# Trunk of two layers: substitution tile in PSUM, six general PSUM banks, products of constants in the heads, and a finish that keeps its split weights

## The chip, the core and the metric

The kernel runs on one core of a Trainium2 chip. PE is the matrix engine (TensorE), DVE the vector engine, ACT the scalar engine, POOL is GpSimd, and SP issues most of the transfers (DMA). Time is device microseconds (us) of one launch. PSUM is the small memory that PE writes its products to, here eight banks of 128 x 512 floats; SBUF is the large working memory. [...]

## The reference, cut to what matters

```
for i in range(2):                                   # two layers
    hx, hc = modulate(rmsnorm(x)), modulate(rmsnorm(ctx))      # 1024 latent, 256 context tokens
    fx, fc = hx @ w_in[i], hc @ w_in[i]
    att_x = softmax attention of 8 heads, 1280 keys            # group A
    y = bidirectional RWKV-7 scan of 8 heads of 64             # group B
        # state = state * w + (state a) b^T + v k^T ;  y = state r
    x = x + gate * (concat(att, rwkv) @ w_out[i])
    x = x + gate * (square(relu(modulate(rmsnorm(x)) @ w_mlp1[i])) @ w_mlp2[i])
return rmsnorm(x, final_g)
```

All numbers are float32. The scan is computed in ten steps of 128 tokens for both directions at once. Within a block of 64 tokens it needs the inverse of 32 unit triangular matrices, whose 32 x 32 parts come out of a forward substitution.

## The kernel before

Each layer has three parts: `phase_in` (input projections, per-token terms), `heads` (the scan and the attention, interleaved) and `phase_out` (output projection and the MLP). In the profile below the heads of layer 0 run from about 504 to 1171 us, those of layer 1 from about 2621 to 3266 us.

**The planner.** Nothing in a part is in hand-written order. Each piece of work is a unit (`us(engine, ns, dependencies, function, ...)`) of the class `Units`, with a duration on its engine, a latency until others may use its result, perhaps a PSUM bank, and the number of PE rows it uses. `run` simulates the engines with these numbers: at each turn it takes, of the units that could start within `slack` of the earliest, the one with the longest path behind it, where `RANKS_HEADS` adds an offset to named kinds of unit. It also models PE's clock, from how much PE was used. The order so found is the order of the instructions on each engine; at run time each engine then runs its queue strictly in that order and waits where an operand is late. So the planner's numbers choose an order and are no times of the chip.

**A bank class** is a list of PSUM tiles that units draw from. Before, the heads have `g` (3 banks: score products, blocks, transposes, small sums), `x` (2: products for the row maxima), `z` (2: the chain of the scan's state) and `o` (1: attention output), together eight.

**The recurrence.** Step i loads `BV` and `AR`, forms blocks on PE (L377) that DVE masks into `A` (L381), transposes tokens (L391, L401), and ACT moves them (`BKt`, `G`). `begin1` to `begin3` lay the 32 triangular matrices out in `AX` and make unit rows in `Y` (`begin2b`, two kinds of POOL memset). The substitution is 31 turns of two DVE instructions: `mult` (L436) writes `tmp` from a column of `AX` and a row of `Y`, `total` (L440) adds `tmp` into `Y`. Each needs the one before. `AX`, `Y` and `tmp` all lie in SBUF. `end1` to `end3` carry the result to `XT`, after which PE and ACT run the chain z, u, s, y (L519 to L562) for each half of a step and direction.

**The attention** takes per head and 512 queries twelve products for the row maxima (L715, reduced by DVE at L717), the negated maximum (L718) spread by PE (L723), ten times three score products (L742), exponentials on ACT (L747), sums on POOL (L751), and products with the values (L736).

**The finish.** The last part of the last layer multiplies the last quarter of hidden units (four weight tiles `R[0]` to `R[3]`) into `x` for the first 512 tokens (a = 1), then for two pieces of 256 (a = 2), and normalises. Weights go to PE as two rounded parts: `split_weights` rounds on ACT (L967) and subtracts the rest on DVE or, for a = 2, on POOL (L969). It does so again for each piece, twelve splits in all. `hh` and `hl`, 16 tiles that hold the split input of the MLP, are idle after the last hidden product.

Of the kernel before, what the change touches and what calls it, by code (L numbers as in the profile page):

```python
# [9 lines left out]
F32 = mybir.dt.float32  # L10
# [89 lines left out]
def sp_ns(n, k=1):  # L100
# [16 lines left out]
class Units:  # L117
# [5 lines left out]
    WINDOW, UP, DOWN = 3413.3, 0.83, 0.47  # L123

    def __init__(self, slack, ranks, latency={}, give_back=True, cold=False, up=UP, down=DOWN, lead=0):
# [37 lines left out]
    def run(self, banks):  # L163
# [21 lines left out]
        while waiting:  # L185
# [11 lines left out]
            ns = u.ns + (u.beside if free.get("Pool", 0.0) > s else 0)  # L197
            if u.eng == "PE":
# [64 lines left out]
class Trunk:  # L263
# [34 lines left out]


    def heads(self, li, ard, bvd, pc, gated, ysd, kd, vd, qd, qrd, krr, catd):  # L300

        with ExitStack() as es:
            e1 = self.pool(es, "hd", 1)
            ps = self.pool(es, "hps", 1, space=PSUM)
            banks = {k: [ps.tile([128, 512], F32, name=f"ps_{k}{j}") for j in range(n)] for k, n in (("g", 3), ("x", 2), ("z", 2), ("o", 1))}
            tiles = {}


            for name, n, shape in (("YF", 1, [128, 32, 32]), ("AX", 1, [128, 32, 32]), ("XM", 1, [128, 32, 32]), ("Y", 1, [128, 32, 16]), ("tmp", 1, [128, 144]),
# [6 lines left out]
            us = Units(59, RANKS_HEADS, dict(PE=120, ACT=75, DVE=75, Pool=75, SP=2300), False, True, 0.745, 0.395, 100)  # L316
# [6 lines left out]
    def recurrence(self, us, tiles, li, ard, bvd, pc, gated, ysd, catd):  # L323
# [9 lines left out]
        YF, XT, XM, tmp, sq, rs8 = (tiles[k][0] for k in ("YF", "XT", "XM", "tmp", "sq", "rs8"))  # L333
# [3 lines left out]
        half = lambda e: slice(64 * e, 64 * e + 64)  # L337
        heads = [(p, e, half(e)) for p in range(4) for e in range(2)]
# [11 lines left out]
        def step(i):  # L350
# [20 lines left out]
            for d in range(2):  # L371
                for ph in range(2):
                    for e in range(2):
# [9 lines left out]
                        x = add(f"blk{d}", us("PE", 772, back(NA, "begin", "m1", "z0", "z1", "y0", "y1"), pe, 284, bank="g", r=[nar[d], nbv[d]], rows=61))  # L383
                        add("A", us("DVE:A", 707, [x], dve, free=x))


            for d in range(2):
                for ph in range(2):
# [7 lines left out]
                    x = add(f"tok{d}", us("PE", 470, [], pe, 213, bank="g", r=[nbv[d]], rows=121))  # L396
# [10 lines left out]
                x = add(f"tok{d}", us("PE", 480, [], pe, 213, bank="g", r=[nbv[d]], rows=121))  # L407
# [3 lines left out]
            for h in range(2):  # L411
                def begin1(h=h):
                    q = slice(32 * h, 32 * h + 32)
                    nc.scalar.copy(YF[q].rearrange("p t n -> p n t"), A[64 + 32 * h:96 + 32 * h, :, 0, q])

                add("begin", us("ACT:begin1", 1970, w["A"] + back(1, "begin2"), begin1))
# [12 lines left out]
            b2 = us("DVE", 1261, w["begin"] + back(NX, "end3"), begin2)  # L429
            b2b = us("Pool", 907, back(NY, "end1"), begin2b)  # L430
# [31 lines left out]
            e2 = add("end2", us("DVE", 1994, e1s + back(1, "m1", "x2"), end2))  # L462
            e2b = add("end2", us("DVE", 1266, e1s, end2b))
            e3b = [add("end3", us("ACT:end3", 1970, [e2b] + back(2, "u0", "u1") + zero, lambda j=j: end3b(j))) for j in (1, 0)]
# [16 lines left out]
            for d in range(2):  # L481
# [9 lines left out]
                x = add("x2", us("PE", 570, [m1a[d], e3b[0]], pe, bank="g", rows=15))  # L491
# [18 lines left out]
            for c in range(2):  # L510
                for d in range(2):
# [52 lines left out]
                    x = add(f"z{d}", us("PE", 567, copies[d] + [az[d]] + w["A"][4 * d:4 * d + 4] + w[f"V{d}"], z_pe, 138, bank="z", rows=121))  # L564
                    zev = us("ACT", 777, [x] + X, z_act, free=x)
                    x = add(f"u{d}", us("PE", 580, [zev, X[d]], u_pe, bank="z", rows=61))
                    uev = us("ACT", 777, [x], u_act, free=x)
                    if i < 9 or c == 0:
                        x = add(f"s{d}", us("PE", 567, [uev] + w[f"BKt{d}"], s_pe, bank="z", rows=121))
                        oldy = [u for u in w.get(f"y{d}", [])] if c else back(1, f"y{d}")  # L570
                        sev = us("DVE", 903, [x] + oldy, s_dve, free=x)
# [8 lines left out]
                    if need:  # L580
                        x = add(f"y{d}", us("PE:yp", 1226, [uev] + sdep, y_pe, bank="z", r=[nar[d]], rows=100))
                        ev = add(f"yev{d}", us("ACT:y" if first else "DVE", 397 if first else 444, [x] + (back(2, "spill", "fin") if first else again), y_ev, free=x))
# [10 lines left out]
        def fin(w, t0, y4, deps, store):  # L593
# [44 lines left out]
            x = us("PE:f1", 562, deps, f1, 570, bank="g")  # L638
            xa = us("ACT:f1a", 1098, [x] + scaled[-1:], f1a, free=x)
            x = us("PE:f2", 900, [xa], f2, 190, bank="g", rows=2)  # L640
            xb = us("ACT", 642, [us("Pool", 1670, [us("DVE", 191, [x], f2a, free=x)], f2b)], f2c)
            x = us("PE", 430, [xb], f3, bank="g", rows=121)
            scaled.append(x)
            xd = us("DVE:f3a", 714, [x], f3a, free=x)
# [9 lines left out]
    def attention(self, us, tiles, li, kd, vd, qd, qrd, krr, catd):  # L654
# [42 lines left out]
        def tile(h, p, q, kh, kl, khk, klk, v, vk, e, t0, tl):  # L697
# [10 lines left out]
            us("ACT", act_ns(tl), [], lambda: nc.scalar.copy(qh[0:96, :tl], raw[:, :tl]), r=[("Qraw", jr)], w=[("Qh", jq)])  # L708
# [16 lines left out]
            x = us("PE:rows", 45 + 111 * nq, [], rows, 170, bank="g", r=[("nm", jq), "identr"], rows=64)  # L725
# [13 lines left out]
            for n in range(nkt):  # L739
# [6 lines left out]
                x = us("PE:scores", 60 + tl * 1.344, [], pe, 212, bank="g", r=khk + klk + [("Qh", jq), ("Qh", jq, "row"), ("Ql", jq), ("Ql", jq, "row")], rows=90)  # L746
# [981 lines left out]
```

## Time and profile before

| | us |
|---|---|
| three timed runs, median (lowest to highest) | 4091.8 (4080.47 to 4091.95) |
| the profiled execution, whole | 4084.27 |
| its span, first to last instruction | 4082.5 |
| PE busy in the span | 3884.9 (95%) |
| DVE, ACT, POOL busy | 2595.6, 1831.8, 1312.9 |
| mean granted PE clock | 0.956 |

The profiled execution lies 7.5 us under the median of the runs and inside their range. PE's busy time is no measure of PE at its best, since matmuls overlap and since the same matmul is longer at the lower clock.

### The profile page before, as it was taken

The page shows a single profiled execution, that of the slowest core. Times are in us where ns is not written, and L with a number is a line of the kernel's source. Part 1 is how long each engine was busy: PE and PEld are TensorE (multiplying, and loading weights), DVE is VectorE, ACT ScalarE, POOL GpSimd, SP SyncE. Part 2 cuts the span into 40 slices and gives each one's busy share as a digit, 9 for nine tenths or more (in the row PEclk, how much of TensorE's full clock was granted, in tenths as well). Part 3 has the DMA queues.
Part 4 walks back from the last instruction along what each step waited for, and adds up shares of the span by engine and source line. Part 5 has one row for each costly group of instructions (what it writes and reads, how often), then busy time and mean ns, then how long its engine had stood idle before and what let it go on. Part 6 is the DMA issues. An engine that isn't in the chain of part 4 may idle for free.

```text
span 4082.5 us, 66855 instructions
## 1 busy us (share of the span) xinstructions
PE 3884.9 (95%) x26144; PEld 2982.8 (73%) x26144; DVE 2595.6 (64%) x4563; ACT 1831.8 (45%) x3113; POOL 1312.9 (32%) x1912
## 2 busy tenths in 40 slices
PE   6999999999999999999998999999999999999998
PEld 3766666766778888888887766766676678777777
DVE  4477277788747455555337477487877565767676
ACT  4355456676644122222115355556676643333333
POOL 1344254545631000000001244455544704333322
PEclk9999979999999999999999999878998999999999
DMA  6256622332342122222103144711232251111111
GB/s 212 73 171 197 222 81 86 97 91 64 92 159 87 58 78 88 78 73 82 37 32 134 58 160 154 237 47 52 81 103 75 69 201 37 52 47 42 52 55 49
DMA packets 279708, 394.21 MB, mean 97 GB/s; under 512 B 60512, under 2 KB 192576, under 8 KB 279392
## 3 DMA queue, kind: packets, MB, share of 16 engines
q1 hardware_dynamic: 278992, 389.36, 30.0%
q8 instruction: 205, 3.36, 0.3%
q14 instruction: 111, 0.91, 0.1%
q10 hardware_dynamic: 400, 0.59, 0.1%
HBM read 288.45 MB, written 101.42 MB: 95 GB/s over the span
## 4 chain that ended last, share of the span: by engine, by line
PE 71%; DVE 14%; ACT 3%; issue 3%; DMA 2%; POOL 1%; SPq 0%; DVEq 0%; POOLq 0%; ACTq 0%
PE qm L930 39%; PE pm_m L930 8%; PE ps_g L742 4%; DVE tmp L436 3%; PE ps_g L377 3%; DVE Y L440 3%; PE ps_o L736 2%; PE ps_x L715 2%; PE qm L943 1%; DVE nm L717 1%; DMA aw<-in_ada_w 1%; PE pm_n L1185 1%; PE ps_z L549 1%; PE ps_z L552 1%; PE ps_z L538 1%
## 5 line engine op out<-in xcount | busy, mean ns | idle before, releaser
L930 PE MATMUL qm<-hh,wh 128*128 128x512 f32 (+1 forms) x1488 | 556.1, 374 | 7.3 <-DVE x L1529 6.9
L930 PE MATMUL qm<-hh,wl 128*128 128x512 f32 (+1 forms) x1488 | 554.2, 372 | 0.7 <-DVE wl L969 0.7
L930 PE MATMUL qm<-hl,wh 128*128 128x512 f32 (+1 forms) x1488 | 554.3, 373 | 0.0
L751 POOL TENSOR_TENSOR Ps<-Ps,P 128x128 f32<-128x128 f32 x1024 | 442.3, 469 | 256.5 <-ACT P L747 255.5
L967 ACT CAST wh<-wr 128x1024 fp32r<-128x1024 f32 x149 | 155.7, 1045 | 440.8 <-PE qm L930 399.2
L930 PE MATMUL pm_m<-hh,wh 128*128 128x512 f32 (+4 forms) x896 | 339.8, 379 | 3.2 <-ACT o L1244 3.2
L930 PE MATMUL pm_m<-hl,wh 128*128 128x512 f32 (+4 forms) x896 | 330.4, 369 | 1.1 <-POOL hl L917 1.1
L930 PE MATMUL pm_m<-hh,wl 128*128 128x512 f32 (+4 forms) x896 | 331.1, 370 | 0.2 <-DVE wl L969 0.2
L930 PEld LDWEIGHTS qm<-hh,wh 128*128 128x128 f32 x1488 | 279.6, 188 | 65.7 <-DVE x L1529 9.0
L930 PEld LDWEIGHTS qm<-hh,wl 128*128 128x128 f32 x1488 | 279.8, 188 | 55.1 <-DVE wl L969 1.4
L930 PEld LDWEIGHTS qm<-hl,wh 128*128 128x128 f32 x1488 | 279.6, 188 | 55.2 <-DVE hl L1425 0.9
L1529 DVE SCALAR_TENSOR_TENSOR x<-qm,mods,x 128x512 f32<-128x512 f32 x280 | 196.5, 742 | 177.1 <-PE qm L930 176.8
L930 PE MATMUL qm<-uh,wl 128*128 128x512 f32 (+1 forms) x768 | 274.0, 357 | 2.1 <-DVE wl L969 2.1
L930 PE MATMUL qm<-uh,wh 128*128 128x512 f32 (+1 forms) x768 | 275.0, 358 | 0.0
L930 PE MATMUL qm<-ul,wh 128*128 128x512 f32 (+1 forms) x768 | 273.8, 357 | 0.0
L969 DVE TENSOR_TENSOR wl<-wr,wh 128x1024 fp32r<-128x1024 f32 x149 | 188.8, 1267 | 127.9 <-ACT wh L967 127.6
L717 DVE TENSOR_REDUCE nm<-ps_x 128x1 f32<-128x512 f32 (+1 forms) x400 | 222.5, 584 | 68.5 <-PE ps_x L715 66.6
L747 ACT ACTIVATE P<-ps_g 128x512 f32<-128x512 f32 (+1 forms) x336 | 192.2, 587 | 140.2 <-PE ps_g L742 118.8
L1452 DVE SCALAR_TENSOR_TENSOR x<-qm,mods,x 128x512 f32<-128x512 f32 x160 | 119.6, 749 | 196.0 <-PE qm L930 192.6
L436 DVE TENSOR_TENSOR tmp<-AX,Y 128x126 f32<-128x126 f32 (+22 forms) x620 | 224.3, 362 | 21.8 <-ACT AX L427 3.7
L440 DVE TENSOR_TENSOR Y<-Y,tmp 128x126 f32<-128x126 f32 (+22 forms) x620 | 212.7, 343 | 22.4
L930 PEld LDWEIGHTS pm_m<-hh,wh 128*128 128x128 f32 (+2 forms) x896 | 169.8, 190 | 67.1 <-issue 31.0
(348 smaller groups left out, 8786.3 us busy)
## 6 DMA issues: line engine op xcount, KB each, us to landing
wr<-in_w SPq DMA_DIRECT2D x90, 512.0 KB, 3.6
BV<-bv SPq DMA_DIRECT2D x40, 768.0 KB, 4.3
raw<-in_ada_w SPq DMA_DIRECT2D x48, 512.0 KB, 3.9
AR<-ar SPq DMA_DIRECT2D x40, 512.0 KB, 5.9
wr<-in_w_in SPq DMA_DIRECT2D x37, 512.0 KB, 3.8
aw<-in_ada_w SPq DMA_DIRECT2D x32, 512.0 KB, 4.2
bv<-bk SPq DMA_DIRECT2D x32, 512.0 KB, 3.1
ar<-ar SPq DMA_DIRECT2D x32, 512.0 KB, 3.8
```

What stands on the lines that cost most here:

```text
L377: nc.tensor.matmul(b[:, 128 * j:128 * j + 128], BK[d][half(e), c, p], AR[d][half(e), 2 * p + c], start=True, stop=True)
L436: nc.vector.tensor_tensor(tm, AX[:, t + 1:32, t:t + 1].to_broadcast(tm.shape), Y[:, t:t + 1, 0:nu].to_broadcast(tm.shape), op=ALU.mult)
L440: nc.vector.tensor_tensor(y, y, tmp[:, 0:ns * nu].rearrange("p (s u) -> p s u", s=ns), op=ALU.add)
L717: us("DVE", 175 + kn * 1.04, [], lambda b, i=i, n=n, kn=kn: nc.vector.tensor_reduce(m3[:, i, n:n + 1], b[:, :kn], AXIS_X, ALU.max), w=[("n ...
L742: nc.tensor.matmul(b[:, :tl], x[:, 128 * n:128 * n + 128], y[:, :tl], start=i == 0, stop=i == 2)
L747: us("ACT", 195 + tl * 0.835, [], lambda b, j=j: nc.scalar.activation(P[j][:, :tl], b[:, :tl], AF.Exp, scale=SCALE), w=[("P", j)], free=x)
L751: us("Pool:sums" if n == 1 else "Pool", 483, [], lambda a=a, b=P[j][:, c:c + 128], c=c: nc.gpsimd.tensor_tensor(sums[:, c:c + 128], a, b, ...
L930: self.nc.tensor.matmul(out, a, b, start=n == 0, stop=n == last)
L967: us("ACT", 947, [], lambda: nc.scalar.copy(wh, raw), r=[key], w=[("wh", j)])
L969: us("Pool" if pool else "DVE:weights", ns, [], lambda: eng.tensor_tensor(wl, raw, wh.bitcast(F32), op=ALU.subtract), r=[key, ("wh", j)], ...
L1452: us("DVE", dve_ns(tl), [u[1]], lambda b: nc.vector.scalar_tensor_tensor(X(m, a), b[:, :tl], self.mods[li][:, 8 * gate + m, s:s + 1], X(m, ...
L1529: z = us("DVE", dve_ns(512), [z], lambda b, m=m, a=a, f=f: nc.vector.scalar_tensor_tensor(X(m, a), b, f, X(m, a), ALU.mult, ALU.add), r=[" ...
```

## The change

1. In the heads `Y` moves to a PSUM bank of its own. Its unit rows are made once, in an SBUF tile `Y0`, and each step copies `Y0` to `Y` on ACT where POOL ran memsets.
2. The banks of `g`, `x` and `z` (seven) become one class `g` of six; every unit of the heads draws from it, save attention output.
3. `filler` multiplies two constant tiles (`ident`, `cmean`) into a free bank of class `g`; nobody reads the product. The planner adds such products wherever it has PE idle for over 500 ns. That comes to 42 of them: 9, 2 and 3 at the start and 2, 1 and 2 at the end of the heads of layer 0; 9, 2 and 3 at the start and 9 at the end of those of layer 1.
4. The planner's durations and latencies in the heads are new, and each layer has its own offsets `RANKS_HEADS[li]`, so the order of both heads is new throughout.
5. In the finish the weights are split once, into `hh[0..3]` and `hl[0..3]`, and the hidden units into `hh[4..7]` and `hl[4..7]`; four splits, all subtractions on DVE.

```diff
+    IDLE, FILL = 500.0, 222.0
...
+            idle = s - free.get("PE", 0.0) if u.eng == "PE" and self.fill else 0
+            if idle > self.IDLE:
+
+                bank, fn = self.fill
+                j = slots[bank].index(min(slots[bank]))
+                n = int((idle - self.IDLE / 2) / (self.FILL * (2 if cold else 1)))
+                if slots[bank][j] <= free.get("PE", 0.0) and n:
+                    fn(banks[bank][j], n)
...
+    def filler(self, b, n):
+
+        for _ in range(n):
+            self.nc.tensor.matmul(b[:, 0:128], self.ident, self.c("cmean"), start=True, stop=True)
...
-            banks = {k: [ps.tile([128, 512], F32, name=f"ps_{k}{j}") for j in range(n)] for k, n in (("g", 3), ("x", 2), ("z", 2), ("o", 1))}
-            tiles = {}
+            banks = {k: [ps.tile([128, 512], F32, name=f"ps_{k}{j}") for j in range(n)] for k, n in (("g", 6), ("o", 1))}
+            tiles = {"Y": [ps.tile([128, 32, 16], F32, name=f"ps_Y{li}")]}
...
-            us = Units(59, RANKS_HEADS, dict(PE=120, ACT=75, DVE=75, Pool=75, SP=2300), False, True, 0.745, 0.395, 100)
+            us = Units(59, RANKS_HEADS[li], dict(PE=110, ACT=20, DVE=115, Pool=80, SP=2300), False, True, 0.745, 0.395, 80, ("g", self.filler))
...
             def begin2b():
-                nc.gpsimd.memset(Y, 0.0)
-                for g in range(2):
-                    nc.gpsimd.memset(Y[half(g)].rearrange("p a b -> p (a b)")[:, 16 * g::33], 1.0)
+                nc.scalar.copy(Y, Y0)
...
-            b2b = us("Pool", 907, back(NY, "end1"), begin2b)
+            b2b = us("ACT", 650, back(NY, "end1") + ones, begin2b)
...
-                prev = [us("DVE:mult", 158 + 1.05 * ns * nu, prev, lambda t=t, ns=ns, nu=nu: mult(t, ns, nu), 0, beside=60)]
-                prev = [us("DVE:total", 158 + 1.05 * ns * nu, prev, lambda t=t, ns=ns, nu=nu: total(t, ns, nu), 0 if t < 30 else None, beside=60)]
+                prev = [us("DVE:mult", 73 + 1.05 * ns * nu, prev, lambda t=t, ns=ns, nu=nu: mult(t, ns, nu))]
+                prev = [us("DVE:total", 73 + 1.05 * ns * nu, prev, lambda t=t, ns=ns, nu=nu: total(t, ns, nu))]
...
             def finish(a, parts):
...
                 if a == 1:
...
+                    for n in range(4):
+                        us("ACT", act_ns(1024), [], lambda n=n: nc.scalar.copy(hh[n].t, R[n]), r=[("r", n)], w=both("hh", n))
+                        us("DVE:weights", dve_ns(1024), [], lambda n=n: nc.vector.tensor_tensor(hl[n].t, R[n], hh[n].t.bitcast(F32), op=ALU.subtract), r=[("r", n)] + both("hh", n), w=both("hl", n))
...
-                        if m % 2 == 0:
-                            wh, wl, wk = self.split_weights(us, R[m // 2], ("r", m // 2), tiles, a == 2)
...
+                        wh, wl, wk = hh[m // 2].t, hl[m // 2].t, both("hh", m // 2) + both("hl", m // 2)
```

Three places show what the new order is; rows that stand for one instruction have its output, its inputs and the output's shape, and the numbers behind the names tell buffers apart.

PE's queue where the heads of layer 0 begin: `ps_g_...` are banks, `ct` holds the constants, L401 and L391 (after: L438 and L428) transpose tokens, L377 (after: L414) forms blocks. Before:

```order
L401 MATMUL ps_g_3470<-ct,BV_3485 128x128 x4
L391 MATMUL ps_g_3471<-ct,BV_3485 128x128 x4
L391 MATMUL ps_g_3472<-ct,BV_3485 128x128 x4
L401 MATMUL ps_g_3470<-ct,BV_3486 128x128 x4
L391 MATMUL ps_g_3471<-ct,BV_3486 128x128 x4
L391 MATMUL ps_g_3470<-ct,BV_3486 128x128 x4
L377 MATMUL ps_g_3472<-AR_3487,BV_3485 128x128 x4
L377 MATMUL ps_g_3471<-AR_3487,BV_3485 128x128 x4
```

And after:

```order
L327 MATMUL ps_g_3470<-ct 128x128 x9
L428 MATMUL ps_g_3470<-ct,BV_3485 128x128 x4
L428 MATMUL ps_g_3471<-ct,BV_3485 128x128 x4
L438 MATMUL ps_g_3472<-ct,BV_3485 128x128 x4
L327 MATMUL ps_g_3473<-ct 128x128 x2
L428 MATMUL ps_g_3473<-ct,BV_3486 128x128 x4
L428 MATMUL ps_g_3474<-ct,BV_3486 128x128 x4
L438 MATMUL ps_g_3475<-ct,BV_3486 128x128 x4
L327 MATMUL ps_g_3470<-ct 128x128 x3
L414 MATMUL ps_g_3470<-AR_3487,BV_3485 128x128 x4
```

The six token products no longer share three banks, so none of them follows a read-out by ACT, and 14 products of constants (L327) stand between them.

DVE's queue where the first substitution of layer 0 begins. Before:

```order
L436 TENSOR_TENSOR tmp_3482<-AX_3479,Y_3481 128x31
L440 TENSOR_TENSOR Y_3481<-Y_3481,tmp_3482 128x31
L717 TENSOR_REDUCE nm_3520<-ps_x_3474 128x1
L717 TENSOR_REDUCE nm_3520<-ps_x_3473 128x1
L436 TENSOR_TENSOR tmp_3482<-AX_3479,Y_3481 128x30
L440 TENSOR_TENSOR Y_3481<-Y_3481,tmp_3482 128x30
```

After, with `ps_Y` the new tile and L471, L475, L752, L753 for L436, L440, L717, L718:

```order
L471 TENSOR_TENSOR tmp_3482<-AX_3479,ps_Y_3477 128x31
L753 TENSOR_REDUCE nm_3518<-nm_3521 128x4
L475 TENSOR_TENSOR ps_Y_3477<-ps_Y_3477,tmp_3482 128x31
L752 TENSOR_REDUCE nm_3522<-ps_g_3473 128x1
L471 TENSOR_TENSOR tmp_3482<-AX_3479,ps_Y_3477 128x30
L752 TENSOR_REDUCE nm_3522<-ps_g_3470 128x1
```

Each instruction of the substitution now has one input in PSUM, and here a reduction stands between a multiplication and its addition.

POOL's queue at the end of the program: `wl` is the low part of a weight tile, `rs` a small tile of the norm. Before:

```order
L1518 TENSOR_TENSOR t_4_26540<-u_3_26555 128x512
L969 TENSOR_TENSOR wl_0_26535<-r_0_26566,wh_0_26534 128x1024
L969 TENSOR_TENSOR wl_2_26517<-r_1_26567,wh_2_26516 128x1024
L969 TENSOR_TENSOR wl_2_26519<-r_2_26568,wh_2_26518 128x1024
L889 TENSOR_TENSOR rs_0_26543<-rs_0_26543,mh 128x4
L969 TENSOR_TENSOR wl_0_26535<-r_3_26569,wh_0_26534 128x1024
```

After:

```order
L1552 TENSOR_TENSOR t_3_26547<-u_2_26562 128x512
L1543 TENSOR_TENSOR r_1_26575<-r_1_26575,r_3_26577 128x1024
L1552 TENSOR_TENSOR t_4_26548<-u_3_26563 128x512
L924 TENSOR_TENSOR rs_0_26551<-rs_0_26551,mh 128x4
L924 TENSOR_TENSOR rs_0_26551<-rs_0_26551,mh 128x2 x2
```

The eight subtractions of weights (four follow the piece shown) have left POOL.

## Rows read from the trace of the kernel before

**Rows 1.** The page: PE's granted clock in 40 slices, in tenths of full speed.

```profile
PEclk9999979999999999999999999878998999999999
```

**Rows 2.** Busy us (instructions) of the engines in the two heads stretches, clock, DMA.

```profile
512.00:1171.00 659.00, 623.03 (x6863) 448.40 (x6862) 503.60 (x1155) 433.19 (x774) 364.75 (x707) 0.92 0.28 84
2631.00:3264.00 633.00, 594.75 (x6404) 425.75 (x6404) 476.79 (x1093) 411.04 (x716) 339.15 (x666) 0.89 0.26 77
```

**Rows 3.** PE's waits in the first heads: us in total, times, longest.

```profile
PE ps_g L723 <- DVE nm L718: 8.5, 3, 4.2
PE ps_x L715 <- DVE nm L717: 6.2, 11, 1.2
```

**Rows 4.** PE's waits in the second heads, same columns.

```profile
PE ps_g L723 <- DVE nm L718: 8.4, 2, 5.3
PE ps_x L715 <- DVE nm L717: 6.7, 7, 2.1
PE ps_z L549 <- DVE S L542: 6.5, 2, 6.1
```

**Rows 5.** Busy us in the first stretch of each heads; PEclk is the clock.

```profile
511.60:556.00 44.40, 43.92 (x161) 33.61 (x162) 32.01 (x71) 17.23 (x22) 17.47 (x15) 0.50 0.37 127
2631.30:2669.00 37.70, 36.98 (x149) 28.17 (x149) 28.48 (x63) 15.24 (x18) 15.21 (x11) 0.55 0.56 182
```

**Rows 6.** PE in order of time: heads' start, then score products at either clock.

```profile
504.67 1.09 PE L401 MATMUL ps_g<-ct,BV 128*128 128x128 f32 x4 [5.28 <-DMA BV<-bv]
...
511.72 1.12 PE L391 MATMUL ps_g<-ct,BV 128*128 128x128 f32 x4 [2.82 <-ACT G L405]
...
545.97 0.63 PE L742 MATMUL ps_g<-Qh,Kl 97*128 97x512 f32 x1
546.39 0.63 PE L742 MATMUL ps_g<-Ql,Kh 97*128 97x512 f32 x1
...
740.16 0.40 PE L742 MATMUL ps_g<-Qh,Kl 97*128 97x512 f32 x1
740.40 0.40 PE L742 MATMUL ps_g<-Ql,Kh 97*128 97x512 f32 x1
```

**Rows 7.** The page's groups of the substitution: busy, mean ns, idle before.

```profile
L436 DVE TENSOR_TENSOR tmp<-AX,Y 128x126 f32<-128x126 f32 (+22 forms) x620 | 224.3, 362 | 21.8 <-ACT AX L427 3.7
L440 DVE TENSOR_TENSOR Y<-Y,tmp 128x126 f32<-128x126 f32 (+22 forms) x620 | 212.7, 343 | 22.4
```

**Rows 8.** DVE in order of time in step 4: start, us.

```profile
762.83 1.20 DVE L436 TENSOR_TENSOR tmp<-AX,Y 128x78 f32<-128x78 f32 x1
764.06 0.24 DVE L440 TENSOR_TENSOR Y<-Y,tmp 128x78 f32<-128x78 f32 x1
...
767.48 2.65 DVE L436 TENSOR_TENSOR tmp<-AX,Y 128x115 f32<-128x115 f32 x1
```

**Rows 9.** POOL in order of time, same stretch.

```profile
762.66 1.27 POOL L632 TENSOR_TENSOR yo<-yo,gt 128x512 f32<-128x512 f32 x1
...
767.07 2.92 POOL L692 TENSOR_TENSOR Kl<-Kraw,Kh 64x1280 fp32r<-64x1280 f32 x1
```

**Rows 10.** DVE line L543: min/median/max ns of its instructions.

```profile
L543 DVE TENSOR_TENSOR S<-S,pc x76: 424/426/2872, 596.8 to 3243.8; 128x256 f32<-128x256 f32 x76
```

**Rows 11.** DVE groups by shape, first heads: one with PSUM input.

```profile
L542 DVE TENSOR_TENSOR S<-ps_z,S 128x256 f32<-128x256 f32 x38 | 15.8, 416 | 9.0 <-PE ps_z L538 8.0 <-ACT P L747 0.5 <-PE ps_x L715 0.4
```

**Rows 12.** DVE groups by shape in the finish.

```profile
L881 DVE TENSOR_TENSOR acc<-acc,t 128x256 f32<-128x256 f32 x13 | 10.2, 784 | 0.3 <-ACT t L880 0.2
...
L1558 DVE SCALAR_TENSOR_TENSOR x<-qm,mods,x 128x512 f32<-128x512 f32 x8 | 6.0, 744 | 2.3 <-PE qm L930 2.3
...
L1495 DVE TENSOR_TENSOR bl<-u,bh 128x512 fp32r<-128x512 f32 x6 | 3.9, 683 | 0.0
```

**Rows 13.** POOL groups in the finish.

```profile
L969 POOL TENSOR_TENSOR wl<-r,wh 128x1024 fp32r<-128x1024 f32 x8 | 19.2, 2405 | 101.9 <-ACT wh L967 101.9
```

**Rows 14.** PE's waits in the finish.

```profile
PE qn L885 <- DVE acc L881: 9.1, 3, 4.3
```

More of the change, by code (lines that the diff above doesn't have):

```diff
@@ L332, in recurrence @@
         ys = ys + self.yo
-        YF, XT, XM, tmp, sq, rs8 = (tiles[k][0] for k in ("YF", "XT", "XM", "tmp", "sq", "rs8"))
+        YF, XT, XM, tmp, sq, rs8, Y0 = (tiles[k][0] for k in ("YF", "XT", "XM", "tmp", "sq", "rs8", "Y0"))
         gt = tiles["gt"]
@@ L337, in recurrence, with unit_rows @@
         half = lambda e: slice(64 * e, 64 * e + 64)
+        def unit_rows():
+            nc.gpsimd.memset(Y0, 0.0)
+            for g in range(2):
+                nc.gpsimd.memset(Y0[half(g)].rearrange("p a b -> p (a b)")[:, 16 * g::33], 1.0)
+        ones = [us("Pool", 907, [], unit_rows)]
         heads = [(p, e, half(e)) for p in range(4) for e in range(2)]
@@ L414, in begin1 @@
                     nc.scalar.copy(YF[q].rearrange("p t n -> p n t"), A[64 + 32 * h:96 + 32 * h, :, 0, q])
-                add("begin", us("ACT:begin1", 1970, w["A"] + back(1, "begin2"), begin1))
+                add("begin", us("ACT:begin1", 1990, w["A"] + back(1, "begin2"), begin1))
             def begin2():
@@ L461, in step @@
             e1s = [add("end1", us("ACT", 681, prev + back(1, "end2"), lambda g=g: end1(g))) for g in range(2)]
-            e2 = add("end2", us("DVE", 1994, e1s + back(1, "m1", "x2"), end2))
-            e2b = add("end2", us("DVE", 1266, e1s, end2b))
-            e3b = [add("end3", us("ACT:end3", 1970, [e2b] + back(2, "u0", "u1") + zero, lambda j=j: end3b(j))) for j in (1, 0)]
+            e2 = add("end2", us("DVE", 2000, e1s + back(1, "m1", "x2"), end2, 35))
+            e2b = add("end2", us("DVE", 1250, e1s, end2b, 35))
+            e3b = [add("end3", us("ACT:end3", 2000, [e2b] + back(2, "u0", "u1") + zero, lambda j=j: end3b(j))) for j in (1, 0)]
             m1a, X = [], []
@@ L489, in act @@
                         nc.scalar.copy(XT[o:o + 32, 16 * d + e:16 * d + 16:2, 32:64], v3(b, a=16)[64 * e:64 * e + 32, 0:8])
-                x = add("x2", us("PE", 570, [m1a[d], e3b[0]], pe, bank="g", rows=15))
+                x = add("x2", us("PE", 615, [m1a[d], e3b[0]], pe, bank="g", rows=15))
                 X.append(us("ACT", 760, [x, e3b[1]], act, free=x))
@@ L580, in step @@
                     if need:
-                        x = add(f"y{d}", us("PE:yp", 1226, [uev] + sdep, y_pe, bank="z", r=[nar[d]], rows=100))
-                        ev = add(f"yev{d}", us("ACT:y" if first else "DVE", 397 if first else 444, [x] + (back(2, "spill", "fin") if first else again), y_ev, free=x))
+                        x = add(f"y{d}", us("PE:yp", 1226, [uev] + sdep, y_pe, bank="g", r=[nar[d]], rows=100))
+                        ev = add(f"yev{d}", us("ACT:y" if first else "DVE", 397 if first else 334, [x] + (back(2, "spill", "fin") if first else again), y_ev, free=x))
             if need and first:
@@ L764, in total @@
                     nc.tensor.matmul(b[:, i:i + 1], Ps[js][:, 128 * i:128 * i + 128], c1, start=True, stop=True)
-            x = us("PE", 45 + 208 * nq, [], total, 180, bank="g", r=[("Ps", js, 128 * i) for i in range(nq)], rows=1)
-            us("DVE", 199, [], lambda b: nc.vector.reciprocal(rc[:, :nq], b[:, :nq]), w=["rc"], free=x)
+            x = us("PE", 845 / 4 * nq, [], total, 145, bank="g", r=[("Ps", js, 128 * i) for i in range(nq)], rows=1)
+            us("DVE", 92, [], lambda b: nc.vector.reciprocal(rc[:, :nq], b[:, :nq]), w=["rc"], free=x)
             us("Pool", 206 + 54 * nq, [], lambda: nc.gpsimd.tensor_copy(rx[:, :nq], rc[:, :nq].unsqueeze(2).to_broadcast([128, nq, 64])), r=["rc"], w=["rx"])
```

92 lines of the change are left out of this document (54 added, 38 removed).

## The prediction

> **What bounds the kernel now.** I read the clock row of the page first: PE has its full clock nearly everywhere but in the slices of the two heads [rows 1]. Then I cut the time by stage. From 512 to 1171 us and from 2631 to 3264 us, the two heads, PE is busy 623 of 659 us and 595 of 633 us, at a mean clock of 0.92 and 0.89 [rows 2]. So the heads, a third of the time, are PE's, with two leaks: 36 and 38 us in which PE waits, and stretches at half the clock. There are only two levels, so a mean of 0.92 over 659 us is 2 x 0.08 x 659 = 105 us at 1.2 GHz, and 0.89 over 633 us is 139 us; 244 us together. What such a microsecond costs is read from two equal score products: they start 0.42 us apart at the low level and 0.24 us apart at the high one [rows 6], so 0.18 of 0.42, or 0.43 of each slow microsecond, would come back: 105 us for all.
>
> Next, whom PE waits for. The long entries name DVE: the negated maximum 8.5 and 8.4 us, the row maxima 6.2 and 6.7, the state update 6.5 in the second heads [rows 3, 4]; 36 us. DVE is busy only 504 and 477 us there [rows 2], so its total load is not the trouble, but single instructions are late. The substitution shows why: `tmp` takes 1.20 us for 78 elements where the addition of the same 78 takes 0.24, and 2.65 us for 115 [rows 8], and each time a POOL instruction that started just before runs until then (762.66 plus 1.27, 767.07 plus 2.92) [rows 9]. Over the whole run the 1240 instructions of the substitution are busy 224.3 + 212.7 = 437 us [rows 7]. Undisturbed they would take less: an instruction with both inputs in SBUF takes 424 ns at its shortest for 256 elements [rows 10] and 683 for 512 [rows 12], so 1.01 ns for an element and 0.165 us fixed. The substitution has 2 x 2856 elements a step in each partition (the sum of (31 - t)(t // 2 + 1), twice) and 20 steps, which makes 1240 x 0.165 + 114,240 x 0.00101 = 320 us. So POOL costs DVE 117 us, in lumps that no order foresees.
>
> **The change, part by part.** *Y in PSUM.* Where one input is in PSUM, POOL does not show: the state update's first half reads PSUM and takes 416 ns in the mean, its second half has two inputs in SBUF and goes from 424 up to 2872 [rows 10, 11]. I therefore take all 117 us out of DVE. The price of PSUM itself: nothing by the same two rows (416 against 424); at most 61 ns an instruction by the finish, where one with a PSUM input takes 744 and one without 683 for 512 elements [rows 12]. No row shows DVE writing PSUM. I take 0, since the pair of equal form and size is the nearer one, and keep 1240 x 0.061 = 76 us of DVE as the other bound.
>
> What this is worth to PE: of the 36 us of waits for DVE I take half, 18 us, because maxima also wait in a long queue. The slow stretches follow waits; after the two starts, below, 166 of the 244 slow microseconds are left, worth 0.43 x 166 = 71 us, and I take four tenths, 28 us. Both factors are choices. Their bounds are nothing, and all of it.
>
> *Six banks and the start.* At the start of layer 0's heads PE waits 5.28 us for `BV`, and then 2.82 us for ACT to read out a bank, because six token products share three banks [rows 6]; the clock then stays down for 44.4 us although PE is busy 43.9 of them, and in layer 1 for 0.9 x 37.7 = 34 us [rows 5]. After, the six products have six banks and products of constants stand in the gaps. If that keeps the clock up, 78 slow microseconds return 0.43 x 78 = 34 us. The blocks that follow are the same and `AR` still has to land, so I take half: 17 us.
>
> *The products of constants.* 42, each a quarter of a group that takes 1.09 us at the low clock [rows 6], so about 11 us if all were in the way. The 5.28 us wait covers nine of them in either layer, the 2.82 us the next five, and those at the ends stand behind the last norm. I take 0; without that cover it is the 11 us.
>
> *ACT for POOL.* Twenty copies of 512 elements at about 0.65 us (the plan's figure) are 13 us for ACT, which is busy 433 of 659 us [rows 2], and each copy can run while the triangles are being laid out. I take 0; in front of the substitution it would cost at most the 13 us.
>
> *The finish.* Eight POOL subtractions of 2.405 us [rows 13] go, and with them eight roundings on ACT. They block DVE: 13 additions of 256 elements take 784 ns instead of 424, which is 4.7 us [rows 10, 12]; PE waits three times, 9.1 us, for that sum of squares [rows 14]. I take 8 us; the bounds are 4.7 and 9.1 plus some of the slow clock that follows, say 12. DVE keeps the four subtractions that it had.
>
> Sum, against the profiled execution of 4084: 18 + 28 + 17 + 8 = 71, so 4013 us. The runs' median lies 7.5 us above that execution; I add 2 for the way between them and forecast 4015 us for the median after.
>
> **The rivals.** *PSUM is dearer.* At 61 ns an instruction DVE wins 117 - 76 = 41 us instead of 117, 35%. The terms of 18, 28 and 17 shrink to 22, so 4084 - 22 - 8 = 4054 us. For it: each instruction waits for the one before, and a write to PSUM is nowhere in the trace. Against: the equal pair [rows 10, 11]. [...]
>
> *The waits only change their name.* If PE's order, and not DVE's lateness, sets the heads, PE's idle time and slow stretches return behind ACT or the transfers, as in the 2.82 us behind ACT [rows 6]. Then only the finish is left: 4076 us, 4070 to 4095 with a new order's luck.
>
> *Slower: banks.* The chain z, u, s, y had two banks that nobody else held; now its 80 + 80 + 76 + 72 = 308 blocks draw on the six that maxima and scores also hold until DVE or ACT has read them. A block that finds all six held waits for about one instruction that reads 512 elements, 0.68 us [rows 12]. The gain of 63 us in the heads is eaten when 63 / 0.68 = 93 of the 308 blocks wait, and at two thirds of them (205, 139 us) the time is 4084 - 8 - 63 + 139 = 4152 us. Against: the planner counts banks, and PE's waits for a bank were short [rows 3].
>
> **How the numbers follow.** The forecast case, 3960 to 4035 us, has 0.56; dear PSUM, 4035 to 4075, has 0.20; new waits, 4070 to 4095, have 0.15; banks have 0.09. All of the leaks closed, 105 + 36 + 8, would be 3935 us, which leaves little below 3955. About 0.06 lies below 3955 and 0.14 above 4085, so 3955 to 4085 is the range; that of the likeliest case alone is 3960 to 4035. What this kernel's measurement can tell from no change is about 0.3%, here 12 us: faster means below 4079.5. The first two cases and some of the third give 0.82, the rest of the third 0.10, slower 0.08.
>
> **What would show it.** `tmp` and `Y` of the substitution with maxima under 0.4 us and a sum near 320 us, against 400 if PSUM is dear. PE's waits for DVE in the heads below 20 us, and the clock there at 0.95. The first 50 us of both heads at full clock if the six banks and the products of constants do their work. No POOL subtraction in the finish and DVE's additions of 256 near 0.42 us. The forecast is wrong if the heads keep their 659 and 633 us with a quiet DVE, or if PE's list of waits names banks of class `g` behind maxima.

## The result, and the profile after

The median went from 4089.7 us (4 runs, 4080.47 to 4091.95) to 3999.5 us (4 runs, 3990.62 to 4004.63): ratio 0.9781, 95% interval 0.9761 to 0.9800, so 2.2% faster. The profiled execution after took 3990.6 us with a span of 3988.8, against 4082.5 before. Cut at four events of PE, the span shows where the 93.7 us went; a head here runs from its first token product to the first product behind it.

| stretch, us | before | after | difference |
|---|---|---|---|
| to the first token product of layer 0 | 504.7 | 505.8 | +1.1 |
| heads of layer 0 | 664.0 | 619.0 | -45.0 |
| between the heads | 1455.0 | 1454.0 | -1.0 |
| heads of layer 1 | 648.8 | 615.1 | -33.7 |
| the rest, with the finish | 810.0 | 794.9 | -15.1 |

The groups of the two lines of the substitution, after; columns are count, then minimum, median and maximum ns:

```profile
L471 DVE TENSOR_TENSOR tmp<-AX,ps_Y x620: 149/257/297, 538.6 to 3110.7; 128x126 f32<-128x126 f32 x15, 128x30 f32<-128x30 f32 x10, 128x78 f32<-128x78 f32 x10, 128x110 f32<-128x110 f32 x10
```

```profile
L475 DVE TENSOR_TENSOR ps_Y<-ps_Y,tmp x620: 179/269/308, 538.8 to 3110.9; 128x126 f32<-128x126 f32 x15, 128x30 f32<-128x30 f32 x10, 128x78 f32<-128x78 f32 x10, 128x110 f32<-128x110 f32 x10
```

Against [rows 7 to 9] the spread is gone: no instruction takes over 308 ns, where the two rows took 1.20 and 2.65 us and the longest 7.21, and the 1240 of them are busy 316 us instead of 437. POOL runs its sums as before (462 ns each in the mean, 469 before).

The windows of the two heads, before and then after; after the length stand PE, weight loads, DVE, ACT and POOL (busy us, instructions), PE's granted clock, DMA share, GB/s:

```profile
504.70:1168.70 664.00, 625.35 (x6877) 450.70 (x6877) 501.30 (x1151) 436.12 (x778) 371.45 (x716) 0.92 0.29 86
2623.60:3272.40 648.80, 601.05 (x6432) 430.96 (x6432) 479.90 (x1097) 419.11 (x728) 347.78 (x671) 0.88 0.27 83
```

```profile
505.80:1124.80 619.00, 600.50 (x6896) 430.64 (x6896) 430.70 (x1151) 438.36 (x788) 359.82 (x690) 0.95 0.31 93
2578.80:3193.90 615.10, 577.30 (x6461) 417.06 (x6461) 426.53 (x1097) 422.95 (x738) 333.87 (x646) 0.92 0.29 88
```

DVE falls from 501 and 480 us to 431 and 427. PE's idle time, the length less its busy time, falls from 38.6 + 47.8 = 86.4 us to 18.5 + 37.8 = 56.3. The time at the low clock, added up from the clock entries of the trace, falls from 107.6 + 153.9 = 261.5 us to 64.9 + 102.4 = 167.3. Every entry is 1.0 or 0.5 of full speed (90 entries before, 66 after). In the trace before, products of 512 columns in a row start 0.427 us apart in the median at 0.5, which is 1.2 columns per ns and all that the 1.2 GHz of the prediction can stand on, and 0.234 us apart at 1.0; the prediction's sums use the half alone. The list of PE's waits after, first the heads of layer 0, then of layer 1 (us in total, times, longest):

```profile
PE ps_g L428 <- DMA BV<-bv: 3.8, 2, 3.2
...
PE ps_g L750 <- ACT Qh L743: 2.2, 2, 1.5
PE ps_o L771 <- DVE ob L795: 1.6, 3, 0.9
...
PE ps_g L750 <- DVE nm L752: 1.1, 5, 0.3
```

```profile
PE ps_g L414 <- DMA AR<-ar: 6.8, 3, 5.3
...
PE ps_g L554 <- ACT G L612: 5.4, 3, 4.0
PE ps_g L750 <- DVE nm L752: 3.6, 11, 1.0
PE ps_g L428 <- DMA BV<-bv: 3.5, 1, 3.5
PE ps_g L584 <- ACT BKt L431: 2.4, 1, 2.4
```

The waits of 8.5, 6.2, 8.4, 6.7 and 6.5 us for DVE [rows 3, 4] are gone or down to 3.6. All waits for DVE in the two heads were 48.6 us and are 13.7. What is left in layer 1 names transfers and ACT: 6.8 for `AR`, 5.4 for `G`. The waits for ACT stay at 24 us in all, and those for transfers go from 16 to 18.

At the finish, PE's wait for the sum of squares [rows 14], DVE's additions [rows 12] and POOL [rows 13], after:

```profile
PE qn L920 <- DVE acc L916: 2.9, 1, 2.9
```

```profile
L916 DVE TENSOR_TENSOR acc<-acc,t 128x256 f32<-128x256 f32 x14 | 5.8, 418 | 1.4 <-ACT acc L912 1.2
```

```profile
L924 POOL TENSOR_TENSOR rs<-rs,mh 128x2 f32<-128x2 f32 (+1 forms) x3 | 2.4, 805 | 110.6 <-DVE rs L923 110.6
```

The additions are at 418 ns instead of 784, POOL has three small instructions, and one wait of 2.9 us stands where three made 9.1.

### The profile page after: what moved, and what is told of

It reads as the page before. It is cut to its first block, busy times and chain, and to the rows that moved or that the text cites. A ratio compares the mean times of both kernels' runs of the same rounds, so it can differ in the third digit from the quotient of the medians.

```text
span 3988.8 us, 67047 instructions
## 1 busy us (share of the span) xinstructions
PE 3835.6 (96%) x26228; PEld 2952.1 (74%) x26228; DVE 2458.7 (62%) x4563; ACT 1830.2 (46%) x3125; POOL 1266.9 (32%) x1850
## 4 chain that ended last, share of the span: by engine, by line
PE 73%; DVE 11%; DMA 3%; ACT 3%; issue 2%; POOL 1%; SPq 0%; DVEq 0%; POOLq 0%; ACTq 0%
PE qm L965 41%; PE pm_m L965 8%; PE ps_g L777 5%; PE ps_o L771 2%; PE ps_g L414 2%; DVE nm L752 2%; PE qm L978 1%; PE ps_g L750 1%; DVE ps_Y L475 1%; DVE tmp L471 1%; PE ps_g L563 1%; PE ps_g L554 1%; PE ps_g L584 1%; PE ps_g L573 1%; PE ps_g L587 1%
## 5 line engine op out<-in xcount | busy, mean ns | idle before, releaser
L786 POOL TENSOR_TENSOR Ps<-Ps,P 128x128 f32<-128x128 f32 x1024 | 433.6, 462 | 271.0 <-ACT P L782 270.6
L752 DVE TENSOR_REDUCE nm<-ps_g 128x1 f32<-128x512 f32 (+1 forms) x400 | 212.0, 581 | 40.8 <-PE ps_g L750 39.8
L965 PEld LDWEIGHTS pm_m<-hl,wh 128*128 128x128 f32 (+2 forms) x896 | 169.4, 189 | 33.6 <-POOL hl L952 2.1
L965 PEld LDWEIGHTS pm_m<-hh,wl 128*128 128x128 f32 (+2 forms) x896 | 169.9, 190 | 30.7 <-issue 0.7
```

Source lines behind the costliest of these rows:

```text
L752: us("DVE", 63 + kn * 1.048, [], lambda b, i=i, n=n, kn=kn: nc.vector.tensor_reduce(m3[:, i, n:n + 1], b[:, :kn], AXIS_X, ALU.max), w=[("n ...
L786: us("Pool:sums" if n == 1 else "Pool", 415, [], lambda a=a, b=P[j][:, c:c + 128], c=c: nc.gpsimd.tensor_tensor(sums[:, c:c + 128], a, b, ...
L965: self.nc.tensor.matmul(out, a, b, start=n == 0, stop=n == last)
```

## The experiments

Theory A is that of the prediction: with Y in PSUM, POOL no longer holds DVE up, PE waits less and keeps its clock. Theory B is the main rival to it as a cause: the common banks, the refitted numbers of the planner, its offsets and the products of constants make the gain, and the place of Y is incidental. The changed kernel and the twelve of the study:

| kernel | median us | ratio to before (interval) |
|---|---|---|
| changed kernel | 3999.5 | 0.9781 (0.9761 to 0.9800) |
| `changed_again` | 3997.2 | 0.9789 (0.9767 to 0.9810) |
| `finish_only` | 4069.6 | 0.9949 (0.9929 to 0.9968) |
| `y_sbuf` | 4172.5 | 1.0206 (1.0182 to 1.0230) |
| `tmp_psum` | 4152.0 | 1.0160 (1.0135 to 1.0184) |
| `no_products` | 4002.0 | 0.9802 (0.9778 to 0.9827) |
| `seven_banks` | 4099.7 | 1.0029 (1.0011 to 1.0047) |
| `six_banks` | 4098.5 | 1.0031 (1.0012 to 1.0050) |
| `one_z_bank` | 4210.3 | 1.0308 (1.0285 to 1.0331) |
| `y_psum_old_classes` | 4182.8 | 1.0231 (1.0207 to 1.0256) |
| `old_numbers` | 4005.9 | 0.9794 (0.9765 to 0.9822) |
| `old_numbers_new_finish` | 3984.9 | 0.9748 (0.9723 to 0.9773) |
| `old_numbers_products` | 3993.7 | 0.9776 (0.9755 to 0.9797) |

**`y_sbuf`**: the changed kernel with one tile moved.

```diff
-            tiles = {"Y": [ps.tile([128, 32, 16], F32, name=f"ps_Y{li}")]}
+            tiles = {}
...
+            ... ("Y", 1, [128, 32, 16]), ...
```

> The changed kernel with Y back in SBUF (ACT still copies the unit rows), PE, DVE, ACT and POOL in the same order. Theory A, that Y in PSUM keeps POOL off DVE and that this is the larger part of the gain in the heads: the substitution goes from 316 us busy back to about 430, PE's waits for DVE from 14 to over 40 us, and the time by 45 to 65 us to some 4055. Theory B, that the six banks, the refitted numbers and the offsets make the gain and the place of Y is incidental: DVE slows as much, but the time rises by under 15 us.

It rose by 173 us, to 2% above the kernel before. The direction is A's; the size is neither's. The row of the multiplication in that kernel, POOL and DVE in order of time at its longest instruction, and the lines of the chain that ended last:

```profile
L471 DVE TENSOR_TENSOR tmp<-AX,Y x620: 163/291/10019, 540.5 to 3297.0; 128x126 f32<-128x126 f32 x15, 128x30 f32<-128x30 f32 x10, 128x78 f32<-128x78 f32 x10, 128x110 f32<-128x110 f32 x10
```

```profile
857.68 7.12 POOL L786 TENSOR_TENSOR Ps<-Ps,P 128x128 f32<-128x128 f32 x17
864.71 0.42 POOL L803 COPY rx<-rc 128x256 f32<-128x256 f32 x1
865.07 3.39 POOL L786 TENSOR_TENSOR Ps<-Ps,P 128x128 f32<-128x128 f32 x8
868.39 1.29 POOL L744 TENSOR_TENSOR Ql<-Qraw,Qh 96x512 fp32r<-96x512 f32 x1
```

```profile
859.71 10.02 DVE L471 TENSOR_TENSOR tmp<-AX,Y 128x31 f32<-128x31 f32 x1 [1.49 <-ACT AX L462]
869.76 0.21 DVE L475 TENSOR_TENSOR Y<-Y,tmp 128x31 f32<-128x31 f32 x1
```

```profile
PE qm L965 39%; PE pm_m L965 8%; DVE tmp L471 5%; DVE Y L475 4%; PE ps_g L777 3%; PE ps_o L771 2%; PE ps_g L414 2%; DVE nm L752 2%; PE ps_g L750 2%; PE qm L978 1%; PE ps_g L563 1%; PE ps_g L573 1%; PE ps_g L554 1%; PE pm_n L1219 1%; PE ps_g L584 1%
```

DVE's multiplication of 31 elements starts at 859.71 while POOL is in a run of sums; POOL then goes from one instruction to the next without a gap, and DVE ends at 869.73, just after POOL's 868.39 + 1.29 = 869.68. The undisturbed one takes 0.2 us. The substitution is busy 470 us instead of 316, and it stands in the chain with 5 + 4%, against 1 + 1% in the changed kernel. PE's idle time in the two heads is 150.6 us (56.3), the low clock lasts 393 us (167). So the new order lives on a quiet DVE: without it, it is worse than the old one. Theory B falls as a whole, since all that it names is still there and the gain is gone; what its parts are worth is asked below. Why it is 173 us and not 45 to 65 is not shown: the order was planned for a quiet DVE, and with the order of `old_numbers` below the place of Y is worth less.

**`tmp_psum`**: which operand has to be in PSUM. The changed kernel with Y in SBUF and `tmp` in the bank.

```diff
-            tiles = {"Y": [ps.tile([128, 32, 16], F32, name=f"ps_Y{li}")]}
+            tiles = {"tmp": [ps.tile([128, 144], F32, name=f"ps_tmp{li}")]}
...
-            ... ("tmp", 1, [128, 144]), ...
+            ... ("Y", 1, [128, 32, 16]), ...
```

> The changed kernel with Y in SBUF and tmp in the PSUM bank instead. The multiplication then has both inputs in SBUF and its output in PSUM, the addition one input in PSUM and its output in SBUF. If the inputs decide: the multiplication stays stretched (over 110 us a head with single ones of microseconds, as with both tiles in SBUF), the addition is clean at 80 us a head, and the time lies between, 4040 to 4130. If any operand in PSUM is enough: both clean, and 4000.

The two lines of the substitution in this kernel:

```profile
L471 DVE TENSOR_TENSOR ps_tmp<-AX,Y x620: 171/298/10018, 534.9 to 3255.0; 128x126 f32<-128x126 f32 x15, 128x30 f32<-128x30 f32 x10, 128x78 f32<-128x78 f32 x10, 128x110 f32<-128x110 f32 x10
```

```profile
L475 DVE TENSOR_TENSOR Y<-Y,ps_tmp x620: 168/257/299, 535.2 to 3255.3; 128x126 f32<-128x126 f32 x15, 128x30 f32<-128x30 f32 x10, 128x78 f32<-128x78 f32 x10, 128x110 f32<-128x110 f32 x10
```

The multiplication has two inputs in SBUF and writes PSUM: up to 10.0 us, 294 us in all. The addition has one input in PSUM and writes SBUF: at most 299 ns, 156 us in all. Here the inputs decide, and writing to PSUM did not shield the multiplication. The time lies between the two kernels that it mixes, nearer to the slow one and above the 4130 us that I expected at most; why so near was not looked into.

**`seven_banks`, `six_banks`, `old_numbers`**: the banks alone, then Y in PSUM on top of them; numbers, offsets and finish are those of before.

```diff
-            banks = {k: [ps.tile([128, 512], F32, name=f"ps_{k}{j}") for j in range(n)] for k, n in (("g", 3), ("x", 2), ("z", 2), ("o", 1))}
+            banks = {k: [ps.tile([128, 512], F32, name=f"ps_{k}{j}") for j in range(n)] for k, n in (("g", 7), ("o", 1))}
```

Every unit that drew from `x` or `z` draws from `g`; `six_banks` has 6 where this has 7. `old_numbers` has the six banks, Y in the eighth, `Y0`, and ACT's copy, as in the change.

> The kernel before with one edit: the banks of its three classes (3 + 2 + 2) are one class of seven; Y stays in SBUF, numbers and finish as before. If the quiet DVE makes the gain: the two heads stay within 20 us of their 664 + 649 us and the time within 0.5% of before. If the banks make a good part of it: 20 to 40 us less than before.

> The kernel before with six banks in one class instead of seven in three; Y stays in SBUF and the eighth bank is unused; numbers and finish as before. It is the kernel with Y in PSUM and old numbers (4006 us) less that one edit. If Y in PSUM makes the gain once the banks are common: 4085 to 4130 us, no faster than before. If it is the six banks: below 4050.

> The kernel before with Y in PSUM (copied by ACT) and six banks in one class, but with the durations, latencies and offsets of before in the planner, without products of constants and with the old finish. Theory A: DVE is quiet, so 35 to 55 us under before, near 4045. Theory B: the order planned with wrong durations waits elsewhere, and less than 15 us is gained, or some is lost.

The common class by itself, with the order that the planner makes for it, loses 0.3%, with seven banks or six. Both times are as Theory A expected; only the first heads of `seven_banks` took 691 us in the profile, 27 more and not within 20. With Y in PSUM on top, the same numbers give 4005.9 us: 0.9794 against 1.0031 is 2.4%, 97 us. That is more than A said and all that the whole change brought. The windows of the two heads, `six_banks` and then `old_numbers`:

```profile
504.70:1192.90 688.20, 629.45 (x6877) 452.46 (x6877) 511.48 (x1151) 436.30 (x778) 372.71 (x716) 0.89 0.28 83
2649.70:3297.60 647.90, 602.14 (x6432) 429.90 (x6432) 486.28 (x1097) 417.96 (x728) 348.21 (x672) 0.87 0.28 83
```

```profile
503.50:1146.00 642.50, 615.85 (x6877) 444.67 (x6877) 437.65 (x1151) 440.32 (x788) 358.78 (x689) 0.91 0.30 89
2603.00:3188.50 585.50, 562.32 (x6433) 402.54 (x6433) 424.23 (x1097) 421.51 (x737) 335.05 (x645) 0.93 0.31 93
```

The heads shrink from 688.2 + 647.9 to 642.5 + 585.5 us, 108 us. PE's idle time falls from 104.6 to 49.8 us, which is 55, and the low clock from 319 to 204 us, 115 us less. At the 0.43 of [rows 6] these are worth 49, at one half 58; 55 and 49 to 58 account for the 108. In this pair half of the gain is waiting, half is clock. It is more than one edit, though: ACT's copy stands for POOL's memsets, and the planner orders both heads anew. The pairs that keep the order of every engine are the changed kernel with `y_sbuf` and with `tmp_psum`. What a new order is worth by itself was not measured; the changed kernel and `old_numbers_new_finish`, two very different orders with a quiet DVE, lie 0.3% apart, far less than 2.4%.

**`y_psum_old_classes`, `one_z_bank`**: Y in PSUM (with `Y0` and ACT's copy) and the three classes kept, where z has to give up a bank, and the same loss of a bank with Y in SBUF.

```diff
-            banks = {k: [ps.tile([128, 512], F32, name=f"ps_{k}{j}") for j in range(n)] for k, n in (("g", 3), ("x", 2), ("z", 2), ("o", 1))}
+            banks = {k: [ps.tile([128, 512], F32, name=f"ps_{k}{j}") for j in range(n)] for k, n in (("g", 3), ("x", 2), ("z", 1), ("o", 1))}
```

> The kernel before with Y in PSUM, copied there by ACT, and the classes kept but for one bank of z that Y takes (3 + 2 + 1); numbers and finish as before. If the quiet DVE makes the gain: 50 to 85 us under before, although the chain z, u, s, y has one bank. If Y needs the common class: under 30 us.

> The kernel before with one bank in class z instead of two; Y stays in SBUF and the eighth bank is unused. Its difference to the kernel with old classes and Y in PSUM (4183 us) is what Y in PSUM is worth where the scan's chain has one bank. If a quiet DVE pays in any order: 4230 to 4280 us. If PE's order behind the one bank sets the time whatever DVE does: 4170 to 4200.

Neither expectation on the first reckoned with a loss: it is 2.3% slower than before, although its substitution is busy 317 us. The second tells why. The lost bank alone costs 3.1%, 124 us, and Y in PSUM takes 0.8 points of that away, some 30 us, which is between what its two expectations had. The windows of the heads of `one_z_bank`, then of `y_psum_old_classes`:

```profile
506.70:1230.40 723.70, 666.08 (x6877) 471.68 (x6877) 521.59 (x1151) 437.19 (x777) 377.38 (x717) 0.87 0.27 79
2685.30:3384.40 699.10, 646.62 (x6433) 448.17 (x6433) 493.33 (x1097) 419.22 (x728) 351.95 (x672) 0.83 0.26 78
```

```profile
505.80:1232.90 727.10, 682.91 (x6876) 482.01 (x6876) 450.25 (x1151) 440.52 (x787) 358.70 (x689) 0.85 0.27 79
2689.60:3381.00 691.40, 653.85 (x6432) 456.27 (x6432) 434.17 (x1097) 423.81 (x737) 335.84 (x645) 0.83 0.26 79
```

In `one_z_bank` PE's idle time is 110 us against 86 before, only 24 more; the low clock lasts 419 us against 262. So a chain on one bank is paid for mostly in clock. With Y in PSUM, PE's waits for DVE fall from 68 to 29 us and its idle time to 82, but the low clock lasts 463 us, and the heads of the two profiled executions come out 4 us apart. The quiet DVE does shorten PE's waits here, and in these two executions the clock takes the gain back, where the medians keep 30 us of it; why it does was not pursued. Whether a bank of `g` or `x` would have been cheaper to give up was not tried.

**`finish_only`**: the kernel before with the new `finish` and the shorter `split_weights` of the change's diff, nothing else.

> The kernel before with the new finish alone; its heads keep their order. The traces of before and after put the span from the last MLP product's start of the finish to the end some 15 us shorter. If the finish is worth what the pair shows, 15 us less than before (ratio 0.9963); if it is worth only what I forecast, 8 us (0.998); if the gain there came with the order of the heads or the clock, nothing.

The rest behind the second heads takes 795.0 us, as in the changed kernel (794.9; before 810.0). The ratio, 0.9949, is 21 us; its interval, 13 to 29 us, takes in the 15 of the trace and not the 8 that I forecast.

**`no_products`**: the order kept, the products of constants left out.

```diff
-        for _ in range(n):
+        for _ in range(0):
```

> The changed kernel without the 42 products of constants, the order of everything else kept. If they keep the clock up at the starts and ends of the heads: the slow stretches at the two starts grow from 24 and 27 us to 40 or more, and the time by 6 to 12 us. If the six banks alone did it: the same time within 3 us, perhaps 2 us shorter.

It cannot be told from the changed kernel (0.9802, intervals overlapping). The first 50 us of each head, in the changed kernel and then without the products:

```profile
505.80:556.00 50.20, 46.78 (x249) 35.75 (x250) 36.42 (x94) 25.75 (x34) 32.04 (x45) 0.76 0.50 155
2578.80:2629.00 50.20, 47.85 (x251) 38.31 (x252) 34.76 (x78) 25.22 (x33) 29.50 (x39) 0.73 0.63 193
```

```profile
505.60:556.00 50.40, 43.69 (x244) 32.21 (x244) 38.04 (x102) 27.86 (x36) 32.47 (x46) 0.84 0.47 156
2579.10:2629.00 49.90, 47.42 (x246) 37.79 (x246) 36.06 (x82) 26.33 (x34) 29.47 (x39) 0.75 0.64 200
```

The clock is no lower without them: 0.84 and 0.75 against 0.76 and 0.73. In the first 51 us the low level lasts 23.9 and 27.3 us with them, 16.3 and 24.9 without, 26.1 and 11.0 in `six_banks`, and 47.6 and 38.4 before. So the common banks, with the order planned for them, hold the clock up at the starts, and the products do not.

**`old_numbers_new_finish`, `old_numbers_products`, `changed_again`**: are the refitted numbers and the products worth anything? The first is `old_numbers` with the new finish. The second adds `fill`, `filler` and the planner's rule, which places 71 products in that plan:

```diff
-            us = Units(59, RANKS_HEADS, dict(PE=120, ACT=75, DVE=75, Pool=75, SP=2300), False, True, 0.745, 0.395, 100)
+            us = Units(59, RANKS_HEADS, dict(PE=120, ACT=75, DVE=75, Pool=75, SP=2300), False, True, 0.745, 0.395, 100, ("g", self.filler))
```

> Y in PSUM, six banks in one class, the planner's durations, latencies and offsets of before, no products of constants, and the new finish. If refitted numbers and products add nothing: 4006 less the 15 us that the finish took out of its own stretch, so some 3991 us, 5 to 10 below the changed kernel. If they are worth what the changed kernel's 3999.5 would need after the two parts, this one is at 4000 or above.

> Y in PSUM, six banks in one class, the new finish and the numbers of before (3985 us), and products of constants wherever that plan has TensorE idle for over 500 ns; 71 of them. If they return clock: 5 to 15 us less than 3985. If they stand in the way or do nothing: 3985 to 4000.

> The changed kernel as it is, on the chip of the other three, for a second ratio to before. If it is the slower one of it and the kernel with old numbers and the new finish (ratio 0.9748), its ratio is again near 0.978; if the two are equal, near 0.975.

The first, at 3984.9 us, is the fastest kernel of the study: 2.5% under before, and 12 to 15 us under the changed kernel by medians. Its interval (up to 0.9773) meets the changed kernel's first one (from 0.9761) and just meets the second (from 0.9767), so that it is faster than before is clear, and that it is faster than the changed kernel is likely. With products it is at 0.9776, no better. So points 3 and 4 of the change brought nothing that can be measured, and perhaps cost a third of a per cent.

## Why the prediction was right

It forecast 4015 us, 3955 to 4085, and the median is 3999.5. Point by point:

**DVE.** 117 us of DVE's time were to go; the substitution lost 437 - 316 = 121. The sum from the fixed and the per-element cost, 320 us, is right to 1%. The choice of 0 for the price of PSUM was right: sixteen elements take 170 to 182 ns in the median, where they took 175 or 176. The rival *PSUM is dearer* is out. At its 61 ns an instruction the substitution would be busy some 396 us, and it is busy 316. What the forecast took to be the cause, that POOL holds up a DVE instruction with two inputs in SBUF and not one with an input in PSUM, `tmp_psum` shows line by line, 10.0 us against at most 0.299.

**Waits for DVE, 18 us.** They fell by 35 us, from 48.6 to 13.7. Idle time as a whole fell by 30, of which some 7 are filled by products of constants; 23 us of real waits. The halving of the visible waits, a choice, was too careful here.

**Slow clock behind the starts, 28 us.** It was 261.5 - 86.0 = 175.5 us and is 167.3 - 51.2 = 116.1: 59 us less, worth 25 at 0.43. The size is right, and luck has a part in it: the four tenths were a choice. That slow stretches follow waits holds for most of them: in the heads before, PE had idle time in the 7 us ahead of 22 of the 27 falls of its clock, and after, ahead of 15 of 20, where about a third of all such stretches have any.

**The starts, 17 us.** The low clock there fell from 86.0 to 51.2 us, worth 15. The size was right, and the share of the cause that I gave to the products of constants was wrong: the six banks do it alone. By the kernel with the banks alone this term has no value of its own either: the starts of `six_banks` are warmer by 49 us and its time is 0.3% longer, so the clock was lost elsewhere. That this term came out is luck.

**The finish, 8 us.** It is 15. The term counted the 9.1 us of waits for the sum of squares, of which 6.2 went, and left out the rest: PE's waits for `x` from the hidden products before it fell from 9.5 to 6.9 us, and three stretches of 3.4 us at the low clock between 3935 and 4065 us are gone, worth 4.4. Against that, the low stretch in which the program ends is 2.5 us longer, which costs 1.1. That makes 12.1 of 15.

**The terms at nothing.** The 42 products are busy 11.8 us in all, as forecast for the case that they are in the way, and leaving them out gains nothing. ACT's twenty copies take 0.59 us each; no run prices them alone.

**The sum.** The forecast took 71 us off the profiled execution, and it lost 93.7: waits, finish and what follows fell short. Idle time (30, with the products standing in it) and clock (94 us, worth 40 to 47) account for 70 to 77 of the 78.7 us in the heads; with 7 us of products counted as work, 8 to 15 us of PE's busy time are unexplained.

**The rivals.** *The waits only change their name*: a little of it is seen in the heads of layer 1, where transfers and ACT now lead the list and 37.8 us of idle time are left. *Slower: banks*: the mechanism is real, and what it costs depends on the class. In the first heads of `six_banks` PE waits once for 8.7 us with a block product (L377) and once for 3.2 us with the state chain (L519) behind a row maximum (L717), which the kernel before never does. In common banks the whole costs 0.3%, some 12 us, and not the 139; one bank less in z costs 124. What the prediction did not say is that the two edits go together: Y in PSUM with a bank of z given up, and the common class without Y in PSUM, are both slower than before, and together they are 2.1% faster. It added them as separate terms, and no run shows such separate gains; that the sum is near is in part luck, since both edits were made at once.

**The signs.** Maxima under 0.4 us, a sum near 320, waits for DVE below 20 us and additions near 0.42 us came. Two signs did not, or not wholly: the clock is 0.95 in the first heads and 0.92 in the second, and the first 50 us of the heads run at 0.76 and 0.73, not at full clock.

## What to carry to other kernels

In this kernel a chain of DVE instructions that read two SBUF operands each was held up by what POOL ran beside it, sums, products and subtractions, for up to 7.21 us before and 10.02 us in `y_sbuf`. Moving the operand that is an input of every link to PSUM removed that (at most 0.308 us), and moving one that is an output of half the links freed only the links that read it (at most 0.299 us, against 10.0 us for the others). Look for it by the spread of equal instructions (minimum against maximum), not by the mean. When a resource is needed for that, one class that all share gave it up here at far less cost (0.3%) than the class with a serial chain (3.1%; the other classes were not tried). Try that first, and time each edit with and without the other before giving it a share of the gain.

## What the runs showed that I had not expected

A blocked DVE instruction need not come free with the end of one POOL instruction: in `y_sbuf` one was held 10.02 us, behind what was left of a run of 25 sums, a copy and a subtraction, so that many finished meanwhile. Nor does it always wait for a gap in POOL's work. In the kernel before, POOL and then DVE:

```profile
765.82 1.28 POOL L709 TENSOR_TENSOR Ql<-Qraw,Qh 96x512 fp32r<-96x512 f32 x1
```

```profile
766.01 1.21 DVE L440 TENSOR_TENSOR Y<-Y,tmp 128x96 f32<-128x96 f32 x1
```

The addition started under the subtraction that ended at 767.10 us and was done at 767.22, although POOL's next subtraction ran from 767.07 to 769.99 [rows 9]. Of the 32 instructions of the substitution there that took over 1 us, 8 ended like this, inside a POOL instruction that had followed without a gap. What decides between the two is open.

PE's clock fell where PE had no idle time just before. The two windows of the changed kernel before and after such a fall, and PE's main lines in the first:

```profile
749.90:756.70 6.80, 6.80 (x147) 5.79 (x146) 6.11 (x25) 5.74 (x12) 6.80 (x7) 1.00 0.46 120
756.70:763.60 6.90, 5.95 (x44) 3.78 (x41) 6.28 (x23) 4.34 (x11) 4.66 (x12) 0.51 0.85 189
```

```profile
L508 PE MATMUL ps_g<-XM,A 32*32 32x32 f32 x64 | 2.2, 238 | 0.0
...
L520 PE MATMUL ps_g<-XT,XM 32*32 32x32 f32 x64 | 1.6, 193 | 0.0
...
L777 PE MATMUL ps_g<-Qh,Kh 97*128 97x512 f32 x4 | 1.6, 412 | 0.0
```

PE is busy 6.80 of 6.80 us at full clock, 128 of its 147 products are 32 x 32, and then it runs at half the clock. Its last idle time, 0.08 us, ended 9 us ahead of the fall. So idle time is not all that goes ahead of a fall in this kernel, and a product of constants in a gap has no place here, where there was no gap.
